# The input projection of a gated-convolution layer as seven half-size products for two output tiles

## The chip, the cores and the metric

One Trainium2 chip, of which the kernel uses one core. The metric is the device time of the core in microseconds (us); lower is better. A profile tells of one execution; the median is taken over several.

## The reference, cut to what matters

Two residual layers act on x, 512 positions of 2048 channels, all in float32, and a last RMSNorm follows. The first layer (delta rule heads beside windowed attention) is the same before and after. The change is in the second:

```python
def shortconv_layer(h, w_in, conv_w, w_out):
    gate_b, gate_c, u, z = jnp.split(h @ w_in, 4, axis=-1)       # w_in: 2048 x 4*3072
    y = gate_b * causal_depthwise_conv(gate_c * u, conv_w)        # 3 taps
    return (y * jax.nn.silu(z)) @ w_out                           # w_out: 3072 x 2048
...
    h = x + hybrid_layer(rmsnorm(x, norm_w[0]), ...)
    h = h + shortconv_layer(rmsnorm(h, norm_w[1]), ...)
    return rmsnorm(h, final_norm_w)
```

Computed are h @ w_in with 12288 output channels, that is 96 tiles of 128, then the gating and the convolution, then the output projection.

## The kernel before, in words

Activations lie transposed, channels on the 128 partitions and the 512 positions along the free dimension, so a tile is 128 x 512. A float32 product is made of three matmuls in the faster fp32r format: each operand is split into a high part (a copy, rounded to fp32r) and a low part (the difference), and hi*hi, hi*lo and lo*hi are added in PSUM (`mm3`, lines 146 to 151; the three matmuls are L148, L149 and L150). The weights are split as they come: SP loads 8 blocks of 128 x 128, 512 KB, into `w_raw` (two buffers), ACT makes `w_hi` (L141), DVE makes `w_lo` (L143; three buffers each). The activations are split once per layer.

The whole program, by TensorE: the first layer's input projection with the attention and delta-rule work in its gaps; its output projection `w1o` (16 tiles of 24 blocks); the second layer's input projection `w2` (24 steps c of four tiles, 16 blocks each: C, u, z, B); its output projection `w2o` (16 tiles of 24 blocks), whose last tile is done in two halves of 256 columns so that the end of the kernel is short.

The order on TensorE is that of the code (`manual_schedule`); small side tasks enter it by estimated times (`Flow`). On the other engines a scheduler orders the instructions by priority at build time, and each engine then works through its own list in order. Weight loads and splits have a raised priority (`SPLIT_AHEAD`), so that they run ahead as far as buffers allow.

In the loop over c (lines 786 to 809) a projected tile is in PSUM when DVE multiplies it by the norm factor `rbc`, forms the convolution, and at the end of a step makes y, which is split at once into `y_hi` and `y_lo` and kept for the output projection. The residual h1 of the first layer's output, needed again at the end, is stored in DRAM (`H1d`). The activations of the second layer are split by `split_x`, nine tiles as they come, the others from a reload during the last tile of `w1o`. No DMA is issued from POOL.

## Time and profile before

| | us |
|---|---|
| median of 3 runs | 2880.93 (2878.38 to 2881.74) |
| the profiled execution, its span | 2882.2 |
| TensorE busy in it | 2854.8 |
| DVE busy | 1429.0 |
| ACT busy | 877.5 |
| the 23 loop steps that the rows below take | 1012.5 |

The profiled execution's span lies 1.3 us above the median of the runs. Busy time of TensorE is modelled (matmuls overlap, each shows 0.39 us where the next one starts after 0.23), so the distance from one start to the next is the cost of a matmul, and the duration isn't. Weight loads (PEld) overlap them.

### The profile page before, as it was taken

To read this page: it belongs to the slowest core of one execution; us is meant where nothing else is said; L and a number is where in the kernel's file an instruction comes from. 1 tells how busy PE (TensorE), PEld (TensorE's weight loads), DVE (VectorE), ACT (ScalarE), POOL (GpSimd) and SP (SyncE) were. 2 spreads that over 40 slices of the span, in tenths; PEclk is the share of its full clock that TensorE was granted. 3 is DMA by queue.
4 is the path that set the end of the run, shared out by engine and by line. 5 is a ranking of instruction groups with operands and counts; after the bars stand their busy time and mean duration, and the time that the engine had idled before them with its cause. 6 is when DMAs were issued, how large, how long until landed. Compare 5 with 4: busy or idle time off the path is not lost.

```text
span 2882.2 us, 33247 instructions
## 1 busy us (share of the span) xinstructions
PE 2854.8 (99%) x13192; PEld 2362.8 (82%) x13192; DVE 1429.0 (50%) x2179; ACT 877.5 (30%) x1483; POOL 78.8 (3%) x130
## 2 busy tenths in 40 slices
...
GB/s 167 179 181 174 92 87 147 89 84 92 86 91 146 103 120 108 103 101 141 130 130 128 95 96 95 95 95 95 95 96 95 99 98 95 95 95 114 114 114 112
DMA packets 135515, 322.19 MB, mean 112 GB/s; under 512 B 38128, under 2 KB 52720, under 8 KB 135104
## 3 DMA queue, kind: packets, MB, share of 16 engines
...
## 4 chain that ended last, share of the span: by engine, by line
PE 95%; DVE 2%; DMA 1%; ACT 1%; issue 1%; SPq 0%; DVEq 0%; POOL 0%; ACTq 0%
PE acc L148 30%; PE acc L150 29%; PE acc L149 29%; PE p L94 2%; PE o_ps L94 1%; PE s_ps L482 0%; PE s_ps L481 0%; PE s_ps L483 0%; DVE w_lo L143 0%; PE vt_ps L98 0%; DVE y_lo L730 0%; PE kk_ps L94 0%; PE x_ps L94 0%; PE t_ps L94 0%; PE p_ps L98 0%
## 5 line engine op out<-in xcount | busy, mean ns | idle before, releaser
L148 PE MATMUL acc<-x_hi,w_hi 128*128 128x512 f32 x3072 | 1229.8, 400 | 1.7 <-DVE cv_raw L316 1.6
L150 PE MATMUL acc<-x_hi,w_lo 128*128 128x512 f32 x3072 | 1205.7, 392 | 5.0 <-DVE w_lo L143 2.8
L149 PE MATMUL acc<-x_lo,w_hi 128*128 128x512 f32 x3072 | 1200.1, 391 | 0.1
L141 ACT ACTIVATE w_hi<-w_raw 128x1024 fp32r<-128x1024 f32 (+2 forms) x494 | 513.1, 1039 | 1535.4 <-PE acc L149 1153.4
L143 DVE TENSOR_TENSOR w_lo<-w_raw,w_hi 128x1024 fp32r<-128x1024 f32 (+2 forms) x494 | 600.4, 1216 | 657.4 <-ACT w_hi L141 656.7
L150 PEld LDWEIGHTS acc<-x_hi,w_lo 128*128 128x128 f32 x3072 | 578.4, 188 | 137.2 <-DVE w_lo L143 5.4
L149 PEld LDWEIGHTS acc<-x_lo,w_hi 128*128 128x128 f32 x3072 | 579.7, 189 | 118.3 <-DVE x_lo L197 0.5
L148 PEld LDWEIGHTS acc<-x_hi,w_hi 128*128 128x128 f32 x3072 | 579.5, 189 | 116.6 <-DVE cv_raw L316 1.8
L148 PE MATMUL acc<-y_hi,w_hi 128*128 128x512 f32 (+1 forms) x792 | 304.5, 384 | 0.0
L150 PE MATMUL acc<-y_hi,w_lo 128*128 128x512 f32 (+1 forms) x792 | 303.4, 383 | 0.0
L149 PE MATMUL acc<-y_lo,w_hi 128*128 128x512 f32 (+1 forms) x792 | 303.4, 383 | 0.0
L149 PEld LDWEIGHTS acc<-y_lo,w_hi 128*128 128x128 f32 x792 | 149.0, 188 | 28.9
L148 PEld LDWEIGHTS acc<-y_hi,w_hi 128*128 128x128 f32 x792 | 149.0, 188 | 28.9
L150 PEld LDWEIGHTS acc<-y_hi,w_lo 128*128 128x128 f32 x792 | 149.0, 188 | 28.7
L320 DVE SCALAR_TENSOR_TENSOR cv<-cv_raw,dcw_sb,cv 128x512 f32<-128x512 f32 x96 | 71.6, 747 | 0.9
L493 ACT ACTIVATE sc<-sc,nb 128x128 f32<-128x128 f32 (+3 forms) x96 | 50.3, 526 | 47.4 <-DVE nb L491 47.2
L793 DVE TENSOR_TENSOR cu<-acc,cr 128x512 f32<-128x512 f32 x24 | 16.6, 692 | 81.8 <-PE acc L150 81.8
L801 DVE TENSOR_TENSOR zrs<-acc,rbc 128x512 f32<-128x512 f32 x24 | 16.6, 692 | 81.8 <-PE acc L150 81.8
L789 DVE TENSOR_TENSOR cr<-acc,rbc 128x512 f32<-128x512 f32 x24 | 16.6, 692 | 78.7 <-PE acc L150 78.7
L808 DVE SCALAR_TENSOR_TENSOR y<-acc,gzs 128x512 f32<-128x512 f32 x24 | 16.6, 692 | 77.3 <-PE acc L150 77.2
L430 DVE TENSOR_TENSOR itmp<-na 128x62 f32<-128x62 f32 (+30 forms) x62 | 52.8, 852 | 0.4
L432 DVE TENSOR_TENSOR na<-na,itmp 128x62 f32<-128x62 f32 (+30 forms) x62 | 52.8, 852 | 0.3
...
## 6 DMA issues: line engine op xcount, KB each, us to landing
w_raw<-in_w_dram SPq DMA_DIRECT2D x380, 512.0 KB, 3.5
w_raw<-in_w1o_dram SPq DMA_DIRECT2D x48, 512.0 KB, 3.6
w_raw<-in_w2o_dram SPq DMA_DIRECT2D x48, 512.0 KB, 3.6
xr<-in_xT_dram SPq DMA_DIRECT2D x16, 256.0 KB, 4.3
KQd<-kq SPq DMA_DIRECT2D x8, 512.0 KB, 5.1
dd<-Gd SPq DMA_DIRECT2D x16, 256.0 KB, 5.0
QKd<-aq SPq DMA_DIRECT2D x16, 256.0 KB, 2.9
kql<-KQd SPq DMA_DIRECT2D x8, 512.0 KB, 3.5
```

The lines of the kernel that those rows point to most:

```text
L94: PE.matmul(o, lhsT, rhs, start=start, stop=stop)
L141: A.activation(hi, raw, AF.Copy)
L143: V.tensor_sub(lo, raw, hi.bitcast(F32))
L148: PE.matmul(acc, hi, xh, start=first, stop=False)
L149: PE.matmul(acc, hi, xl, start=False, stop=False)
L150: PE.matmul(acc, lo, xh, start=False, stop=last)
L320: V.scalar_tensor_tensor(cv, raw[:, j:j + T], dcw_sb[:, ci, j:j + 1], cv, op0=ALU.mult, op1=ALU.add)
L430: V.tensor_tensor(tv, na[:, j:j + 1, j + 1:64].to_broadcast([P, j, w]), na[:, 0:j, j:j + 1].to_broadcast([P, j, w]), op=ALU.mult)
L432: V.tensor_tensor(na[:, 0:j, j + 1:64], na[:, 0:j, j + 1:64], tv, op=ALU.add)
L493: A.activation(scs[g], scs[g], AF.Exp, bias=nb, scale=SCALE, accum_out=den[:, g:g + 1])
L789: V.tensor_tensor(cr, acc, rbc2, op=ALU.mult)
L793: V.tensor_tensor(cu[:, 2:T + 2], acc, cr, op=ALU.mult)
```

## The change

The second layer's input projection is done for two output tiles at a time by Strassen's scheme in the form with 15 additions. The contraction is cut in two halves (even and odd blocks of 128 channels: `halves` in the host's layout), the positions in two halves of 256, and the two output tiles are the third pair. Seven products of 8 blocks with 256 columns replace two of 16 blocks with 512. Each product is again three matmuls (hi*hi, hi*lo, lo*hi).

For the activations, `forms` makes seven combinations of the four quadrants of a pair of tiles and splits each into hi and lo: 56 tiles in all, made once. Those of the block pairs 0 to 2 are made as the output projection of the first layer yields its tiles, of 3 to 6 during its last two tiles from a reload, of the last one at its end; the last two tiles are therefore computed together, block by block. For the weights, five raw tiles per pair are loaded; two of the four sums (s1, s3) are made by a transfer from POOL that adds into the loaded tile, two (on q11, on q12) by DVE. The seven weight matrices are split as before. Eight raw buffers replace two. Three PSUM tiles take the products, and DVE and ACT copy or add the parts out.

The 56 forms take the places in which y was kept (`xp` and `x2p`), and the six new raw buffers take the place of the y tiles of the first layer. So y is stored in DRAM (`Y2d`) and read back and split behind the loop, all but the last. The tap product of line 795 goes from DVE to ACT.

```diff
-NX2 = 9
+NX2 = 24
+NJ1 = 3
+NRAW = 6
...
+    Y2d = dram.tile([NCH, P, T], F32, name="Y2d")
...
-    xs2 = [None] * KT
...
-                    for k in range(KT - NX2):
-                        hr = op1.tile([P, T], F32, name="hr")
-                        SP.dma_start(hr, H1d[k])
-                        xs2[k] = split_x(*PX, hr, k, 1)
...
-            accA = proj(w2[0], xs2)
...
-                acc = accA if c == 0 else proj(w2[4 * c], xs2)
-                cr = sc.tile([P, T], F32, name="cr", tag="crz")
-                V.tensor_tensor(cr, acc, rbc2, op=ALU.mult)
-                acc = proj(w2[4 * c + 1], xs2)
-                cu = sc.tile([P, T + 2], F32, name="cu")
-                G.memset(cu[:, 0:2], 0.0)
-                V.tensor_tensor(cu[:, 2:T + 2], acc, cr, op=ALU.mult)
-                cv = sc.tile([P, T], F32, name="cvs")
-                V.tensor_scalar(cv, cu[:, 0:T], scw_sb[:, c, 0:1], None, op0=ALU.mult)
-                for j in range(1, 3):
...
-                ys.append(split_y(PX if c < NX2 or c >= NX2 + 12 else PYA if c < NX2 + 4 else PYD, yt))
+    slots = iter([(x2p, "x2", NX2)] * NX2 + [(xp, "x", 32)] * 32)
+    fm = [[None] * NJ for _ in range(7)]
+
+    def form(i, j, src):
+        pool, tag, bufs = next(slots)
+        t = pool.tile([P, 2, H], F32R, name="fm", tag=tag, bufs=bufs)
+        A.activation(t[:, 0, :], src, AF.Copy)
+        V.tensor_tensor(t[:, 1, :], src, t[:, 0, :].bitcast(F32), op=ALU.subtract)
+        fm[i][j] = (t[:, 0, :], t[:, 1, :])
+
+    def forms(pool, j, he, ho):
+        e1, e2, o1, o2 = he[:, 0:H], he[:, H:T], ho[:, 0:H], ho[:, H:T]
+        form(0, j, e1)
+        fa, fb = (pool.tile([P, H], F32, name=n) for n in ("fa", "fb"))
+        V.tensor_tensor(fa, e1, e2, op=ALU.subtract)
+        V.scalar_tensor_tensor(fb, fa, -1.0, o2, op0=ALU.mult, op1=ALU.subtract)
+        form(5, j, fb)
+        form(4, j, fa)
+        fc, fd = (pool.tile([P, H], F32, name=n) for n in ("fa", "fb"))
+        V.tensor_tensor(fc, e2, o2, op=ALU.subtract)
+        form(6, j, fc)
+        form(1, j, o1)
+        form(2, j, o2)
+        V.tensor_tensor(fd, o1, fb, op=ALU.add)
+        form(3, j, fd)
+
...
+            if m < 2 * NJ1 or m >= KT - 2:
+                scaled(m, h1)
+                if m % 2:
+                    forms(op1, m // 2, hs[m - 1], hs[m])
...
+        last = (KT - 2, KT - 1)
+        rxs = [residual(m) for m in last]
+        accs = [new_acc() for _ in last]
+        for c in range(KO // CK):
+            with tc.high_priority(offset=SPLIT_AHEAD):
+                ws = [load_split(wp, w1o[m][:, c * CK:(c + 1) * CK, :], CK) for m in last]
+            for i in range(CK):
+                k = c * CK + i
+                flow.poll()
+                for acc, (hi, lo) in zip(accs, ws):
+                    mm3(acc, hi[:, i, :], lo[:, i, :], ys[k], k == 0, k == KO - 1)
+        for j in range(NJ1, NJ - 1):
+            for m in (2 * j, 2 * j + 1):
+                hr = op1.tile([P, T], F32, name="hr", tag="hr")
+                SP.dma_start(hr, H1d[m])
+                scaled(m, hr)
+            forms(op1, j, hs[2 * j], hs[2 * j + 1])
+        for m, acc, rx in zip(last, accs, rxs):
+            made(m, acc, rx)
...
+    yds.close()
+    with tc.tile_pool(name="w4", bufs=1) as w4, tc.tile_pool(name="sc", bufs=1, side="right") as sc:
+
+        def raw():
+            i = nraw[0]
+            nraw[0] += 1
+            pool, tag, bufs = ((wp, "w_raw", 2), (w4, "w_raw4", NRAW))[i % (2 + NRAW) >= 2]
+            return pool.tile([P, NJ, P], F32, name="w_raw", tag=tag, bufs=bufs)
+
+        nraw = [0]
+
+        def split_w(src):
+            hi = wp.tile([P, NJ, P], F32R, name="w_hi", tag="w_hi", bufs=3)
+            A.activation(hi, src, AF.Copy)
+            lo = wp.tile([P, NJ, P], F32R, name="w_lo", tag="w_lo", bufs=3)
+            V.tensor_sub(lo, src, hi.bitcast(F32))
+            return hi, lo
+
+        def product(w, f, o, first):
+            hi, lo = w
+            o = o[:, 0:H]
+            for j in range(NJ):
+                flow.poll()
+                xh, xl = fm[f][j]
+                PE.matmul(o, hi[:, j, :], xh, start=first and j == 0, stop=False, skip_group_check=not first)
+                PE.matmul(o, hi[:, j, :], xl, start=False, stop=False, skip_group_check=not first)
+                PE.matmul(o, lo[:, j, :], xh, start=False, stop=j == NJ - 1, skip_group_check=not first)
+                flow.t += 0.36
+
+        def pair(wa, wb, c1, c2):
+            with tc.high_priority(offset=SPLIT_AHEAD):
+                q11, s1, s3, q12, q22 = (raw() for _ in range(5))
+                SP.dma_start(s1, wb[:, 0:NJ, :])
+                G.dma_start(s1, wb[:, NJ:KT, :], accum_op=ALU.add)
+                SP.dma_start(q11, wa[:, 0:NJ, :])
+                SP.dma_start(s3, wa[:, 0:NJ, :])
+                G.dma_start(s3, wb[:, 0:NJ, :], accum_op=ALU.add)
+                SP.dma_start(q12, wa[:, NJ:KT, :])
+                SP.dma_start(q22, wb[:, NJ:KT, :])
+            a, b, c = new_acc(), bank("sb"), bank("sc")
+            with tc.high_priority(offset=SPLIT_AHEAD):
+                w = split_w(q11)
+            product(w, 0, a, True)
+            a1 = sc.tile([P, H], F32, name="a1", bufs=2)
+            A.activation(a1, a[:, 0:H], AF.Copy)
+            with tc.high_priority(offset=SPLIT_AHEAD):
+                V.tensor_tensor(q11, q11, s1, op=ALU.add)
+                w = split_w(q11)
+            product(w, 5, b, True)
+            e = sc.tile([P, H], F32, name="e", bufs=2)
+            V.tensor_tensor(e, b[:, 0:H], a1, op=ALU.add)
+            with tc.high_priority(offset=SPLIT_AHEAD):
+                w = split_w(s3)
+            product(w, 6, c, True)
+            with tc.high_priority(offset=SPLIT_AHEAD):
+                w = split_w(s1)
+            product(w, 4, b, False)
+            b2 = sc.tile([P, H], F32, name="b2", bufs=1)
+            V.tensor_tensor(b2, b[:, 0:H], a1, op=ALU.add)
+            V.tensor_tensor(c2[:, H:T], c[:, 0:H], b2, op=ALU.subtract)
+            with tc.high_priority(offset=SPLIT_AHEAD):
+                w = split_w(q12)
+            product(w, 1, a, False)
+            A.activation(c1[:, 0:H], a[:, 0:H], AF.Copy)
+            with tc.high_priority(offset=SPLIT_AHEAD):
+                V.tensor_tensor(q12, q12, q11, op=ALU.add)
+                w = split_w(q12)
+            product(w, 2, b, False)
+            V.tensor_tensor(c1[:, H:T], b[:, 0:H], a1, op=ALU.add)
+            with tc.high_priority(offset=SPLIT_AHEAD):
+                w = split_w(q22)
+            product(w, 3, c, False)
+            V.tensor_tensor(c2[:, 0:H], c[:, 0:H], e, op=ALU.subtract)
...
+            pair(w2[4 * c], w2[4 * c + 1], cc, u)
+            if c == 0:
+                flow.drain()
+                V.tensor_tensor(rbc2, rbc, rbc, op=ALU.mult)
+            V.tensor_tensor(u, u, cc, op=ALU.mult)
+            V.tensor_tensor(u, u, rbc2, op=ALU.mult)
+            A.activation(cc, cu[:, 0:T], AF.Copy, scale=scw_sb[:, c, 0:1])
+            for j in range(1, 3):
+                V.scalar_tensor_tensor(cc, cu[:, j:j + T], scw_sb[:, c, j:j + 1], cc, op0=ALU.mult, op1=ALU.add)
+            V.tensor_tensor(cc, cc, rbc, op=ALU.mult)
+            cz, cb = ctile(), ctile()
+            pair(w2[4 * c + 2], w2[4 * c + 3], cz, cb)
+            V.tensor_tensor(cz, cz, rbc, op=ALU.mult)
+            gz = sc.tile([P, T], F32, name="gzs")
+            A.activation(gz, cz, AF.Tanh, scale=0.5)
+            V.scalar_tensor_tensor(gz, gz, 1.0, cz, op0=ALU.add, op1=ALU.mult)
+            V.tensor_tensor(gz, gz, cc, op=ALU.mult)
+            yt = sc.tile([P, T], F32, name="y2", bufs=2)
+            V.scalar_tensor_tensor(yt, cb, 0.5, gz, op0=ALU.mult, op1=ALU.mult)
+            if c < NCH - 1:
+                SP.dma_start(Y2d[c], yt)
+        ys = [None] * NCH
+        for c in range(NCH):
+            if c < NCH - 1:
+                yl = sc.tile([P, T], F32, name="yl", tag="ct", bufs=6)
+                SP.dma_start(yl, Y2d[c])
+            else:
+                yl = yt
+            ys[c] = split_y(PX if c < 16 else (x2p, "x2", NX2), yl)
...
+    halves = np.arange(DM).reshape(KT // 2, 2, P).transpose(1, 0, 2).reshape(-1)
+    w2 = mtiles(sc_w_in[0][halves], np.concatenate(```

The order of instructions shows it at three places. First DVE within one step of the loop, from the step's first operation on, as it was; `w_lo` are the weight splits, L789 to L798 the pointwise work:

```order
L789 TENSOR_TENSOR cr<-acc,rbc_12703 128x512 [waits PE_49]
L143 TENSOR_TENSOR w_lo<-w_raw,w_hi 128x1024 [waits DMAHW3_49,Activation_49]
L143 TENSOR_TENSOR w_lo<-w_raw,w_hi 128x1024 [waits DMAHW4_49,PE_49,Activation_49]
L793 TENSOR_TENSOR cu<-acc,cr 128x512 [waits DVE_49,PE_49]
L795 TENSOR_SCALAR cvs<-cu,scw_sb 128x512 [waits DVE_49,Pool_49]
L143 TENSOR_TENSOR w_lo<-w_raw,w_hi 128x1024 [waits DMAHW5_49,Activation_49]
L797 SCALAR_TENSOR_TENSOR cvs<-cu,scw_sb,cvs 128x512 [waits DVE_49] x2
L798 TENSOR_TENSOR cvs<-cvs,rbc 128x512 [waits DVE_49]
```

And DVE now, in a pair that follows one of C and u, from the combination that waits for the pair before to the sixth product's weights; L888 to L910 are combinations of products, `ct` the tiles they make, L903 the sum of weights on DVE:

```order
L910 TENSOR_TENSOR ct<-sc,e 128x256 [waits PE_49]
L853 TENSOR_TENSOR w_lo<-w_raw,w_hi 128x1024 [waits DMASW7_49,Activation_49]
L924 TENSOR_TENSOR ct<-ct 128x512 [waits DVE_49]
L925 TENSOR_TENSOR ct<-ct,rbc_12831 128x512 [waits DVE_49]
L853 TENSOR_TENSOR w_lo<-w_raw,w_hi 128x1024 [waits PE_49,Activation_49]
L928 SCALAR_TENSOR_TENSOR ct<-ct,scw_sb 128x512 [waits Activation_49]
L888 TENSOR_TENSOR e<-sb,a_13590 128x256 [waits PE_49]
L928 SCALAR_TENSOR_TENSOR ct<-ct,scw_sb 128x512 [waits DVE_49]
L853 TENSOR_TENSOR w_lo<-w_raw,w_hi 128x1024 [waits DMAHW2_49,Activation_49]
L929 TENSOR_TENSOR ct<-ct,rbc 128x512 [waits DVE_49]
L903 TENSOR_TENSOR w_raw<-w_raw 128x1024 [waits DVE_49]
L896 TENSOR_TENSOR b_13679<-sb,a_13590 128x256 [waits PE_49]
```

The splits now stand between operations that wait for single products (PE in the brackets), and two of a pair's splits stand behind a transfer of POOL (DMASW).

Second SP's queue where the loop is entered. It was, from the last reloads of h1 on:

```order
L139 DMA w_raw<-in_w_dram 128x1024 [waits DMAHW2_49,DVE_49]
L768 DMA hr<-H1d 128x512 [waits DMAHW6_49,DMAHW1_49,DVE_49]
L775 DMA H1d<-h_12614 128x512 [waits DVE_49]
L139 DMA w_raw<-in_w_dram 128x1024 [waits DMAHW5_49,DVE_49]
L139 DMA w_raw<-in_w_dram 128x1024 [waits DMAHW0_49,DVE_49]
```

It is now (L870 to L876 are the loads of s1, q11, s3, q12 and q22 of the first pair and the next):

```order
L142 DMA w_raw<-in_w1o_dram 128x1024 [waits DMAHW4_49,DVE_49]
L870 DMA w_raw<-in_w_dram 128x1024 [waits DMAHW5_49,DVE_49]
L831 DMA hr<-H1d 128x512 [waits DMAHW2_49,Activation_49]
L872 DMA w_raw<-in_w_dram 128x1024 [waits DMAHW4_49,DVE_49]
L873 DMA w_raw<-in_w_dram 128x1024 [waits PE_49]
L875 DMA w_raw<-in_w_dram 128x1024
L876 DMA w_raw<-in_w_dram 128x1024
L870 DMA w_raw<-in_w_dram 128x1024 [waits DMAHW3_49]
```

The load of s3 (L873) waits for TensorE, whose reads of the first layer's y end there, and the loads behind it wait with it.

Third DVE where the loop is left. It was (L804 to L808 end the last step, L820 is the first output tile's sum):

```order
L805 TENSOR_TENSOR gzs<-gzs,cvs 128x512 [waits DVE_49]
L143 TENSOR_TENSOR w_lo<-w_raw,w_hi 128x1024 [waits DMAHW0_49,PE_49,Activation_49]
L808 SCALAR_TENSOR_TENSOR y_19022<-acc,gzs 128x512 [waits DVE_49,PE_49]
L143 TENSOR_TENSOR w_lo<-w_raw,w_hi 128x1024 [waits DMAHW1_49,Activation_49]
L730 TENSOR_TENSOR y_lo<-y_19022,y_hi 128x512 [waits Activation_49]
L143 TENSOR_TENSOR w_lo<-w_raw,w_hi 128x1024 [waits DMAHW2_49,PE_49,Activation_49]
L143 TENSOR_TENSOR w_lo<-w_raw,w_hi 128x1024 [waits DMAHW3_49,PE_49,Activation_49]
L820 TENSOR_TENSOR h_19136<-acc,rx_19043 128x512 [waits DMAHW4_49,DVE_49,PE_49]
```

It is now (`yl` are tiles read back; L910 waits for the last product):

```order
L734 TENSOR_TENSOR y_lo<-yl,y_hi 128x512 [waits DMAHW2_49,Activation_49]
L734 TENSOR_TENSOR y_lo<-yl,y_hi 128x512 [waits DMAHW3_49,Activation_49]
L910 TENSOR_TENSOR ct<-sc,e 128x256 [waits PE_49]
L146 TENSOR_TENSOR w_lo<-w_raw,w_hi 128x1024 [waits DMAHW4_49,Activation_49]
L935 SCALAR_TENSOR_TENSOR gzs<-gzs,ct 128x512 [waits Activation_49]
L734 TENSOR_TENSOR y_lo<-yl,y_hi 128x512 [waits DMAHW5_49,Activation_49]
L936 TENSOR_TENSOR gzs<-gzs,ct 128x512 [waits DVE_49]
L734 TENSOR_TENSOR y_lo<-yl,y_hi 128x512 [waits DMAHW7_49,Activation_49]
L734 TENSOR_TENSOR y_lo<-yl,y_hi 128x512 [waits DMAHW0_49,Activation_49]
L938 SCALAR_TENSOR_TENSOR y_24005<-ct,gzs 128x512 [waits DVE_49]
L734 TENSOR_TENSOR y_lo<-yl,y_hi 128x512 [waits DMAHW2_49,Activation_49]
```

Three y tiles are split before L910, one of them above the piece shown; the other 21 stand behind it.

## Rows read from the trace of the kernel before

**Rows 1.** The page: busy time of each engine, and the chain that ended last, by engine
```profile
PE 2854.8 (99%) x13192; PEld 2362.8 (82%) x13192; DVE 1429.0 (50%) x2179; ACT 877.5 (30%) x1483; POOL 78.8 (3%) x130
PE 95%; DVE 2%; DMA 1%; ACT 1%; issue 1%; SPq 0%; DVEq 0%; POOL 0%; ACTq 0%
```

**Rows 2.** Windows, the 23 steps of the layer's loop: busy us, clock, DMA share, GB/s
```profile
1558.60:2571.10 1012.50, 1012.50 (x4417) 829.94 (x4416) 388.49 (x434) 218.49 (x229) 2.29 (x23) 1.00 0.29 96
```

**Rows 3.** Line 789, first op of each loop step: count, ns min/median/max, first and last start
```profile
L789 DVE TENSOR_TENSOR cr<-acc,rbc x24: 691/692/692, 1558.6 to 2571.1; 128x512 f32<-128x512 f32 x24
```

**Rows 4.** Waits in 1640 to 2640 us: SP's queue, then DVE (us, times, longest)
```profile
SPq L139 <- DVE w_lo L143: 917.9, 182, 5.4
DVE w_lo L143 <- ACT w_hi L141: 311.4, 160, 4.3
DVE cu L793 <- PE acc L150: 74.9, 22, 3.4
```

**Rows 5.** Timeline of TensorE, 256-column products of the last output tile, 20 L148 starts
```profile
2852.77 0.28 PE L148 MATMUL acc<-y_hi,w_hi 128*128 128x256 f32 x1
...
2859.61 0.28 PE L148 MATMUL acc<-y_hi,w_hi 128*128 128x256 f32 x1
```

**Rows 6.** Timeline of TensorE, 512-column products, eight L148 starts: start us, us
```profile
2839.98 0.39 PE L148 MATMUL acc<-y_hi,w_hi 128*128 128x512 f32 x1
...
2844.74 0.39 PE L148 MATMUL acc<-y_hi,w_hi 128*128 128x512 f32 x1
```

**Rows 7.** Windows, the 256-column stretch: busy us of PE, PEld, DVE, ACT, POOL
```profile
2853.00:2859.00 6.00, 6.00 (x52) 6.00 (x51) 0.42 (x1) 0.82 (x2) 0.00 (x0) 1.00 0.01 3
```

**Rows 8.** Groups by shape, DVE and ACT: xcount, busy us, mean ns of one, idle before
```profile
L143 DVE TENSOR_TENSOR w_lo<-w_raw,w_hi 128x1024 fp32r<-128x1024 f32 x476 | 582.6, 1224 | 656.9 <-ACT w_hi L141 656.2
L141 ACT ACTIVATE w_hi<-w_raw 128x1024 fp32r<-128x1024 f32 x476 | 504.8, 1061 | 1534.1 <-PE acc L149 1152.6 <-issue 346.0 <-DMA w_raw<-in_w_dram 7.2
L370 DVE TENSOR_TENSOR aq<-kk,dd 128x1024 f32<-128x1024 f32 x16 | 18.9, 1218 | 0.4 <-ACT kk L359 0.4
L797 DVE SCALAR_TENSOR_TENSOR cvs<-cu,scw_sb,cvs 128x512 f32<-128x512 f32 x48 | 36.0, 749 | 0.8
L798 DVE TENSOR_TENSOR cvs<-cvs,rbc 128x512 f32<-128x512 f32 x24 | 16.6, 692 | 0.8
L730 DVE TENSOR_TENSOR y_lo<-y,y_hi 128x512 fp32r<-128x512 f32 x24 | 16.4, 685 | 0.8 <-ACT y_hi L728 0.8
L651 DVE TENSOR_TENSOR vs<-p,c 128x256 f32<-128x256 f32 x24 | 10.1, 423 | 19.5 <-PE p L94 19.4
L498 DVE TENSOR_TENSOR sc<-sc,sc 128x256 f32<-128x256 f32 x24 | 9.9, 414 | 0.0
L654 ACT ACTIVATE vn<-p 128x256 f32<-128x256 f32 x32 | 12.3, 383 | 63.3 <-DVE vs L651 52.2 <-PE p L94 11.0
L803 ACT ACTIVATE gzs<-zrs 128x512 f32<-128x512 f32 x24 | 15.0, 625 | 0.0
```

**Rows 9.** DMA issues: KB each, median us from issue to landing
```profile
w_raw<-in_w_dram SPq DMA_DIRECT2D x380, 512.0 KB, 3.5
T11d<-itmp SPq DMA_DIRECT2D x4, 512.0 KB, 6.2
yl<-YBd SPq DMA_DIRECT2D x8, 256.0 KB, 3.1
hr<-H1d SPq DMA_DIRECT2D x7, 256.0 KB, 3.9
```

**Rows 10.** Groups, the longest operation of POOL
```profile
L223 POOL TENSOR_TENSOR ssq<-ssq,sq 128x512 f32<-128x512 f32 x16 | 23.7, 1480 | 17.9 <-ACT sq L222 17.7
```

**Rows 11.** Windows around the one long pause of TensorE between its large products
```profile
863.00:868.00 5.00, 2.40 (x17) 1.82 (x15) 2.77 (x4) 1.54 (x2) 0.65 (x3) 0.93 0.23 70
868.00:873.00 5.00, 5.00 (x12) 3.94 (x13) 4.21 (x11) 1.26 (x2) 0.32 (x2) 0.50 0.95 311
```

75 lines of the change are left out of this document (35 added, 40 removed).

## The prediction

> **What bounds the kernel now.** I read the page first: TensorE is busy 99% of the span, and the chain that ended last lies on PE for 95% of it [rows 1]. Then the windows over the loop that the change rewrites: in 1012.5 us TensorE has no idle time at all, DVE is busy 388 us, ACT 218 us, POOL 2 us, the DMA engines 29% [rows 2]. The first operation of a loop step starts at 1558.6 us for the first and at 2571.1 us for the last of 24 steps [rows 3], so a step takes 1012.5 / 23 = 44.02 us, for 4 x 48 = 192 matmuls of 512 columns: 0.2293 us each. The reader is to see in the waits that the others wait for TensorE or for one that does: SP's loads for DVE to free the raw weights, 917.9 us in all, DVE for ACT's weight splits and for the products' ends [rows 4]. So in this loop the time is the number of matmuls times the step from one to the next, and nothing else ends last. All 24 steps cost 24 x 44.02 = 1056.5 us.
>
> **The change part by part.**
>
> *The products.* Each two output tiles took 2 x 48 matmuls of 512 columns; now seven products of 8 x 3 matmuls of 256 columns, 168. In all 4608 matmuls go and 48 x 168 = 8064 come. What a half-width matmul costs is shown by the last output tile, which is done in two halves: from the first to the last of 20 starts of line 148, 57 matmuls apart, 6.84 us, 0.1200 us each [rows 5]. The 512-column ones of the output projection take 4.76 / 21 = 0.2267 us [rows 6]. So half the columns cost 53% of the time, not 50%, and of Strassen's eighth (7/8) only 7/8 x 2 x 0.1200 / 0.2267 = 0.926 is left. 8064 x 0.1200 = 967.7 us. The stretch of rows 5 has DVE, ACT and DMA nearly idle, and its weight loads fill all 6.00 of 6.00 us [rows 7]; in the loop they will be busy. The nearest row for that: the loop's 512-column step is 0.2293 [rows 2], where the output projection's is 0.2267 [rows 6], 1.15% more. With that share on top it is 978.9 us. I take the middle, 973.3 us. The gain on TensorE is 1056.5 - 973.3 = 83.2 us, 77.6 to 88.8.
>
> *Does DVE keep up?* Per pair of tiles DVE now has seven w_lo splits of 1024 elements at 1.224 us, two weight sums of that size at 1.218, five combinations of 256 columns at 0.423, and half of a step's pointwise work: seven operations of 512 columns at 0.69 and two multiply-adds at 0.749 [rows 8]. That is 8.57 + 2.44 + 2.12 + 3.16 = 16.3 us, against 168 x 0.1207 = 20.3 us of TensorE: 80%, where it was 38%. ACT: 7 x 1.061 + 2 x 0.383 + 0.625 = 8.8 us, 43% [rows 8]. Both are covered, if the order of the queues lets them run ahead. I followed DVE's order through one pair with those durations, from the end T of the pair before. Weight buffers are three, so product n's split begins when product n-3 ends (products take 2.9 us). The w_lo of the third product is ready at T + 2.3 and wanted at T + 5.8; the fourth 5.2 and 8.7; the fifth 8.3 and 11.6; the seventh 14.8 and 17.4; the next pair's first two 16.7 and 20.3, 20.3 and 23.2. The tightest is the sixth, whose weights are summed on DVE only after the fifth's split: split, line 929, sum, ACT's copy, line 896, split end at T + 13.2, wanted at T + 14.5. Even that has 1.3 us. Cost in the loop: nothing, covered by TensorE; if the cover goes, see the second rival.
>
> *The loads.* Per pair seven transfers of 512 KB in place of four, two of them adding into their target from POOL's queue, plus half a store of y: 3.8 MB per 20.3 us, 188 GB/s (96 now [rows 2]). An adding transfer isn't in this trace. Lower bound: a plain load, 3.5 us to landing; upper: that load plus the slowest 512 KB row, 3.5 + 6.2 = 9.7 us [rows 9]; what POOL needs to issue one is bounded by nothing and its longest operation, 1.48 us [rows 10]. I take 6.2 us plus 1.5. The raw buffers are eight for five per pair: s1 of a pair may load some 24 us before it is needed, s3 26 us, q12 and q22 17 us or more before. Load plus adding, 3.5 + 7.7 = 11.2 us (14.7 at the upper bound), hides in that, and two per pair fit in 20.3 us even one after the other.
>
> *Entering the loop* costs TensorE, since it was seamless before. Let T be the end of the last output-projection matmul. (a) The first product has seven of eight k-blocks ready, 21 x 0.12 = 2.5 us of cover. For the eighth DVE still does, in its order, two residual adds (0.69 each, the first from T - 0.5), one w_lo, two adds into ssq and four operations of 256 columns: 1.38 + 1.22 + 1.37 + 1.66 - 0.5 = 5.1 us [rows 8], so 2.6 us late. (b) The third product's weights s3 lie where the pool of y tiles was, whose last reader is the projection's last block: the load is issued at T, lands at T + 3.8, the adding one at T + 11.5, split T + 13.8; wanted at T + 2.6 + 5.8 = 8.4. 5.4 us late. (c) The last two projection tiles run interleaved with three weight buffers for pairs: at the first border the second tile's split is ready about 0.6 us late. (d) Such pauses can halve the clock: after 2.6 idle us in 863 to 868 us the granted clock stood at 0.50 (1.2 GHz) for the next 5 us [rows 11]; that would cost about 2.5 us here. Together 11 us.
>
> *Leaving the loop.* The y tiles no longer split as they come; 23 are stored and read back, since their place is held by the forms until the last product. DVE's order puts three of them before the last product's combination, so behind it 21 splits at 0.685, four operations of the last step and three w_lo come to 14.4 + 2.5 + 3.7 = 20.6 us [rows 8], and three matmuls, 0.7 us, follow the last of them. The first output tile takes 72 x 0.2267 = 16.3 us when nothing holds it: 5 us late. Reloading (3.1 to 3.9 us each [rows 9], at first three buffers) adds perhaps 1 us. Together 6 us.
>
> The forms' other work (77 operations of 256 columns on DVE, 0.414 each [rows 8]) lies beside the output projection, where TensorE ends last; nothing is charged.
>
> Sum: 2882.2 (profiled span) - 83.2 + 11 + 6 = 2816.0. The median of the runs shown, 2880.93, is 1.3 us under that span, so 2814.7; I say 2815. The forecast's own range: gain 77.6 to 88.8, ends together 5 to 30 us (both late sums hidden by work done earlier, or both doubled by the clock): 2797 to 2833.
>
> **The rivals.**
> 1. *The adding loads become the bound* (slower). Everything in a pair waits for s1 and s3. If POOL's queue does its two adding transfers one after the other and one takes x us, a pair takes at least 2x. The change breaks even when a pair loses (83.2 - 17) / 48 = 1.38 us, at 21.65 us: x = 10.8 us decides. At 13 us, 26 per pair, the kernel ends at 2815 + 48 x 5.7 = 3089 us. For: no adding transfer and no DMA of POOL is in the trace. Against: the upper bound of 9.7 us from rows 9, and 0.95 of DMA share was reached at 311 GB/s [rows 11]. Chance 8%. The Trainium skill, "SBUF — State Buffer", section "Who interferes with whom", would raise it: the descriptors of a transfer issued from POOL can't be written while DVE runs an operation that takes both of its ports, as copies and tensor_scalar do. By the same section tensor_tensor takes no such mode, and the loop's one tensor_scalar, line 795, became ACT's line 926; no run here shows either.
> 2. *DVE becomes the bound in the loop.* If its operations come 30% slower beside twice the DMA traffic and POOL's transfers, 16.3 us become 21.2 a pair, 0.9 us over TensorE's, lost 48 times: 2815 + 43 = 2858 us. For: it is busy 80%, in order, and waits for TensorE within each pair. Against: the margins above, and 1.3 us of the tightest one is not eaten by less than a third. Chance 9%.
> 3. *Half-width matmuls are slower among busy engines*, by 5%: 0.126 us, 1016 us, the gain 40: 2858 us. For: weight loads fill rows 7. Against: with twice the columns the load made 1.15%. Chance 5%.
> 4. *Half the columns cost half*, 0.1133 us [rows 6]: 914 us, 2815 - 59 = 2756 us. For: nothing but arithmetic. Against: rows 5, at the full granted clock of 1.00 [rows 7]. Chance 4%. The Trainium skill, "TensorE: Matmul & The Clock Gate", section "Back-to-back issue gap", goes further, columns / 2.4 GHz + 2.5 ns, an estimate of 109.2 ns for 256 columns, and the loop would take 881 us; the trace's 120 ns disagree, and the measurement decides.
>
> **How the numbers follow.** Forecast 74%, rivals 8, 9, 5 and 4%. Low end: 2795, just under the forecast's best case, which leaves rival 4 out. High end: 2860, which takes in rivals 2 and 3 at their prices and leaves out 1. What a measurement can tell from no change is 0.2%, 5.8 us. Faster by more than that: 74 + 9 + 5 + 4 = 92%, less 2 for rivals 2 and 3 at double price, 90%; within 0.2%: 2%; slower: 8%.
>
> **What would show it.** TensorE's starts 0.120 to 0.1215 us apart within a product, the loop's step at 40.5 us from one line 924 to the next, PE without waits inside the loop, DVE near 80% there. Idle time of TensorE before the first and third product of the first pair, and in the first output tile, line by line behind y_lo. Wrong would be: PE waiting for w_hi or w_lo in every pair (rival 2), DVE or ACT waiting for an adding transfer in every pair (rival 1), or starts over 0.125 us apart (rival 3).

## The result and the profile after

2818.02 us, median of 4 runs (2814.83 to 2821.60), against 2881.34 for the kernel before in the same comparison: a ratio of 0.9783, interval 0.9769 to 0.9797. The forecast was 2815, so the sum came out. Its terms did not: the gain on TensorE was larger, and so was what entering and leaving the loop cost, by nearly as much. That the two errors cancelled is luck.

The stages show it. They are cut at TensorE's first matmul on a y tile, its first of the second layer's input projection and its first of the second output projection (timelines of both traces; us):

| stage | before | after | moved by | forecast |
|---|---|---|---|---|
| up to the first y matmul | 1277.39 | 1276.46 | -0.9 | 0 |
| first output projection | 268.21 | 273.50 | +5.3 | part of the entry's +11 |
| input projection, 24 steps | 1058.37 | 976.61 | -81.8 | -83.2, and the rest of the +11 |
| from the first y matmul after it to the end | 278.19 | 293.27 | +15.1 | +6 |
| span | 2882.16 | 2819.84 | -62.3 | -66 |

The page's busy times and its chain answer to [rows 1]: TensorE is busy 98% of the span and is still what ends last, with 93% of that chain; DVE is at 64% for 50, and POOL's work has doubled by issuing adding loads.

```profile
PE 2774.8 (98%) x16648; PEld 2463.6 (87%) x16648; DVE 1798.9 (64%) x2707; ACT 1091.6 (39%) x1803; POOL 160.6 (6%) x226
PE 93%; DVE 3%; DMA 2%; issue 1%; ACT 1%; SPq 0%; DVEq 0%; POOL 0%; ACTq 0%; POOLq 0%
```

The window over the changed loop, from line 924 of the first step to that of the last (columns as in [rows 2]), and the starts of that line, which answer to [rows 3]:

```profile
1586.70:2508.90 922.20, 922.20 (x7730) 922.20 (x7730) 713.07 (x853) 395.01 (x460) 80.07 (x112) 1.00 0.71 190
```

```profile
L924 DVE TENSOR_TENSOR ct<-ct x24: 685/686/690, 1586.7 to 2508.9; 128x512 f32<-128x512 f32 x24
```

TensorE never waits there; its weight loads are full now too, DVE is at 77%, the DMA engines at 71% where they were at 29%. A step takes 922.2 / 23 = 40.10 us for 336 matmuls, 0.1193 us each: below the 0.1200 that I had as the lower bound. 8064 of these are 962.3 us; the stage's other 14.3 us lie at its start. In 1600 to 2500 us the others wait for TensorE or for one that does, as in [rows 4]:

```profile
ACT w_hi L851 <- PE acc L863: 156.8, 87, 1.8
DVE w_lo L853 <- ACT w_hi L851: 141.4, 202, 1.5
```

DVE's operations kept their lengths, and an adding load takes 7.1 us in the middle; these answer to [rows 8, 9, 10], first the groups of the loop by shape, then the issues (KB, median us to landing), then what an adding load takes POOL to issue:

```profile
L853 DVE TENSOR_TENSOR w_lo<-w_raw,w_hi 128x1024 fp32r<-128x1024 f32 x308 | 376.9, 1224 | 139.8 <-ACT w_hi L851 138.1
L884 DVE TENSOR_TENSOR w_raw<-w_raw 128x1024 f32<-128x1024 f32 x44 | 53.9, 1225 | 1.5
L896 DVE TENSOR_TENSOR b<-sb,a 128x256 f32<-128x256 f32 x44 | 18.6, 422 | 38.1 <-PE sb L864 38.1
```

```profile
w_raw<-in_w_dram SPq DMA_DIRECT2D x428, 512.0 KB, 4.4
w_raw<-in_w_dram POOLq DMA_DIRECT2D x96, 512.0 KB, 7.1
Y2d<-y SPq DMA_DIRECT2D x23, 256.0 KB, 5.3
yl<-Y2d SPq DMA_DIRECT2D x23, 256.0 KB, 4.4
```

```profile
L871 POOL DMA_DIRECT2D w_raw<-in_w_dram x48: 857/862/1056, 1533.6 to 2476.7; - x48
```

At the entry all of TensorE's waits, 1515 to 1575 us (us, times, longest), and then windows behind the pauses, the first behind that at the border, the others from the first product on (the granted clock is the third number from the end):

```profile
PE sc L862 <- ACT w_hi L851: 5.5, 1, 5.5
PE acc L151 <- ACT w_hi L144: 1.6, 1, 1.6
PE acc L863 <- DVE fm L769: 1.3, 1, 1.3
PE acc L153 <- DVE w_lo L146: 1.2, 2, 0.9
PE sc L864 <- DVE w_lo L853: 0.5, 1, 0.5
PE acc L862 <- ACT fm L768: 0.3, 1, 0.3
```

```profile
1525.00:1530.00 5.00, 3.83 (x11) 2.71 (x12) 5.00 (x12) 4.88 (x12) 0.00 (x0) 0.76 0.58 189
1550.00:1560.00 10.00, 8.42 (x56) 8.02 (x55) 7.04 (x17) 4.84 (x12) 1.06 (x2) 0.83 0.84 273
1560.00:1570.00 10.00, 4.07 (x18) 3.57 (x18) 4.21 (x5) 3.33 (x4) 2.75 (x4) 0.76 1.06 256
1570.00:1580.00 10.00, 10.00 (x79) 10.00 (x78) 4.88 (x7) 3.94 (x5) 0.86 (x1) 0.90 0.88 273
```

The waits are those forecast: the third product for s3 (L862 into sc), the eighth block of forms (L768, L769), the border of the interleaved tiles (L151, L153). What the 5.5 us are made of, the chain of waits says (start, us): the load of s3, issued when the projection ends, and the adding load behind it, 9.79 us beside five other loads at a DMA share of 1.06, then ACT's split.

```profile
1550.15 4.14 DMA w_raw<-in_w_dram
...
1554.83 9.79 DMA w_raw<-in_w_dram
...
1564.70 1.06 ACT w_hi L851
1565.79 1.24 DVE w_lo L853
```

At the exit, 2526 to 2555 us, waits of TensorE and of ACT:

```profile
PE acc L152 <- DVE y_lo L734: 3.5, 7, 0.9
PE acc L151 <- ACT y_hi L732: 3.2, 4, 1.3
```

```profile
ACT y_hi L732 <- DMA yl<-Y2d: 9.0, 6, 3.0
```

TensorE waits for splits of y, as forecast, but the splits wait 9.0 us for reloads. That is another cause than mine, which was DVE's turn; experiment 4 tells the two apart.

### The profile page after: what moved, and what is told of

Its sections match the earlier page's. It is cut to its first block, busy times and chain, and to the rows that moved or that the text cites. A ratio compares the mean times of both kernels' runs of the same rounds, so it can differ in the third digit from the quotient of the medians.

```text
span 2819.8 us, 41852 instructions
## 1 busy us (share of the span) xinstructions
PE 2774.8 (98%) x16648; PEld 2463.6 (87%) x16648; DVE 1798.9 (64%) x2707; ACT 1091.6 (39%) x1803; POOL 160.6 (6%) x226
## 3 DMA queue, kind: packets, MB, share of 16 engines
q0 software_dynamic: 13824, 50.34, 10.1%
## 4 chain that ended last, share of the span: by engine, by line
PE 93%; DVE 3%; DMA 2%; issue 1%; ACT 1%; SPq 0%; DVEq 0%; POOL 0%; ACTq 0%; POOLq 0%
PE acc L151 17%; PE acc L153 17%; PE acc L152 17%; PE sb L862 5%; PE sb L864 5%; PE sb L863 5%; PE sc L862 3%; PE sc L864 3%; PE acc L862 3%; PE acc L864 3%; PE sc L863 3%; PE acc L863 3%; PE p L96 2%; DMA w_raw<-in_w_dram 1%; DVE w_lo L146 1%
## 5 line engine op out<-in xcount | busy, mean ns | idle before, releaser
L151 PE MATMUL acc<-x_hi,w_hi 128*128 128x512 f32 x1536 | 622.5, 405 | 1.6 <-DVE cv_raw L319 1.6
L153 PE MATMUL acc<-x_hi,w_lo 128*128 128x512 f32 x1536 | 602.3, 392 | 5.1 <-DVE w_lo L146 5.1
L152 PE MATMUL acc<-x_lo,w_hi 128*128 128x512 f32 x1536 | 600.6, 391 | 0.5 <-DVE x_lo L200 0.3
L144 ACT ACTIVATE w_hi<-w_raw 128x1024 fp32r<-128x1024 f32 (+2 forms) x302 | 308.9, 1024 | 683.9 <-PE acc L152 513.9
L851 ACT ACTIVATE w_hi<-w_raw 128x1024 fp32r<-128x1024 f32 x336 | 356.3, 1061 | 559.2 <-PE acc L863 165.8
L146 DVE TENSOR_TENSOR w_lo<-w_raw,w_hi 128x1024 fp32r<-128x1024 f32 (+2 forms) x302 | 363.6, 1206 | 315.1 <-ACT w_hi L144 314.4
L853 DVE TENSOR_TENSOR w_lo<-w_raw,w_hi 128x1024 fp32r<-128x1024 f32 x336 | 411.0, 1224 | 160.9 <-ACT w_hi L851 159.0
L153 PEld LDWEIGHTS acc<-x_hi,w_lo 128*128 128x128 f32 x1536 | 289.2, 188 | 69.6 <-DVE w_lo L146 7.2
L151 PEld LDWEIGHTS acc<-x_hi,w_hi 128*128 128x128 f32 x1536 | 290.1, 189 | 57.4 <-DVE cv_raw L319 1.8
L152 PEld LDWEIGHTS acc<-x_lo,w_hi 128*128 128x128 f32 x1536 | 290.3, 189 | 55.8 <-DVE x_lo L200 1.8
L862 PE MATMUL sb<-fm,w_hi 128*128 128x256 f32 x1152 | 325.9, 283 | 0.0
L864 PE MATMUL sb<-fm,w_lo 128*128 128x256 f32 x1152 | 325.2, 282 | 0.0
L863 PE MATMUL sb<-fm,w_hi 128*128 128x256 f32 x1152 | 324.5, 282 | 0.0
L151 PE MATMUL acc<-y_hi,w_hi 128*128 128x512 f32 (+1 forms) x792 | 307.6, 388 | 4.8 <-ACT y_hi L732 3.2
L152 PE MATMUL acc<-y_lo,w_hi 128*128 128x512 f32 (+1 forms) x792 | 305.7, 386 | 3.5 <-DVE y_lo L734 3.5
L153 PE MATMUL acc<-y_hi,w_lo 128*128 128x512 f32 (+1 forms) x792 | 305.8, 386 | 1.2 <-DVE w_lo L146 1.2
L862 PE MATMUL sc<-fm,w_hi 128*128 128x256 f32 x768 | 218.0, 284 | 5.5 <-ACT w_hi L851 5.5
L862 PEld LDWEIGHTS sb<-fm,w_hi 128*128 128x128 f32 x1152 | 219.7, 191 | 0.0
L863 PEld LDWEIGHTS sb<-fm,w_hi 128*128 128x128 f32 x1152 | 218.9, 190 | 0.0
L864 PEld LDWEIGHTS sb<-fm,w_lo 128*128 128x128 f32 x1152 | 218.5, 190 | 0.0
L864 PE MATMUL sc<-fm,w_lo 128*128 128x256 f32 x768 | 217.5, 283 | 0.5 <-DVE w_lo L853 0.5
L863 PE MATMUL acc<-fm,w_hi 128*128 128x256 f32 x768 | 216.0, 281 | 1.3 <-DVE fm L769 1.3
## 6 DMA issues: line engine op xcount, KB each, us to landing
w_raw<-in_w_dram SPq DMA_DIRECT2D x428, 512.0 KB, 4.4
w_raw<-in_w_dram POOLq DMA_DIRECT2D x96, 512.0 KB, 7.1
w_raw<-in_w1o_dram SPq DMA_DIRECT2D x48, 512.0 KB, 3.6
w_raw<-in_w2o_dram SPq DMA_DIRECT2D x48, 512.0 KB, 3.6
Y2d<-y SPq DMA_DIRECT2D x23, 256.0 KB, 5.3
yl<-Y2d SPq DMA_DIRECT2D x23, 256.0 KB, 4.4
xr<-in_xT_dram SPq DMA_DIRECT2D x16, 256.0 KB, 4.3
KQd<-kq SPq DMA_DIRECT2D x8, 512.0 KB, 5.1
```

Source lines behind the costliest of these rows:

```text
L144: A.activation(hi, raw, AF.Copy)
L146: V.tensor_sub(lo, raw, hi.bitcast(F32))
L151: PE.matmul(acc, hi, xh, start=first, stop=False)
L152: PE.matmul(acc, hi, xl, start=False, stop=False)
L153: PE.matmul(acc, lo, xh, start=False, stop=last)
L851: A.activation(hi, src, AF.Copy)
```

## The experiments

Each was made from the changed kernel, the first from the kernel before. Stage lengths are cut as above.

**1. Half-width matmuls with the old placement and traffic.**

```
-                mm3(acc, hi[:, j, :], lo[:, j, :], xs[k], ...)
+                for s in (slice(0, 256), slice(256, 512)):
+                    PE.matmul(acc[:, s], hi[:, j, :], xh[:, s], ...)  # hi*xl, lo*xh alike
```

> The kernel before, with each 512-column matmul of the second input projection (line 148 to 150) done as two of 256 columns: 9216 in place of 4608, all else as before, and the result the same. It prices the half-width step with the old placement of the operands and the old traffic. Theory A (the shape sets it; what made the 512-column step 0.2297 us in this loop doesn't touch half-width ones): 9216 x 0.1193 = 1099.5 us for the loop in place of 1058.4, the span 2882 + 41 = 2923 us, PEld full. Rival (the loop's share of 1.15% goes on top, as half of my sum had it): 9216 x 0.1214 = 1118.8 us, the span 2943 us.

This kernel does not keep the result, and its first tile stays at 512 columns; the other 9120 matmuls are as said. The stage took 1096.39 us, the span 2918.2 us (timed once: 2919.94): theory A. Inside the loop a matmul takes 1000 / 8418 = 0.1188 us, with DVE, ACT and DMA as busy as in the kernel before:

```profile
1600.00:2600.00 1000.00, 1000.00 (x8418) 1000.00 (x8417) 370.20 (x414) 207.47 (x217) 2.19 (x22) 1.00 0.28 93
```

The 1.15% that the 512-column step had in this loop doesn't touch the half-width one. From start to start the step is 120.0 ns for the blocks of activations in xp and 117.8 for those in x2p, as in the changed kernel.

**2. Without the adding loads.**

```
-                G.dma_start(s1, wb[:, NJ:KT, :], accum_op=ALU.add)
...
-                G.dma_start(s3, wb[:, 0:NJ, :], accum_op=ALU.add)
```

> The changed kernel without its two accumulating loads per pair: s1 and s3 are only loaded, so the weight sums are left out and the products are those of other weights. Theory A (the adding loads cost only at the first pair, where s3 waits for load plus adding load): the idle 5.75 us before the first pair's third product shrinks to under 0.5 us, the clock there stays higher, the loop's step stays at 40.1 us, the span falls from 2819.8 to 2810 us, give or take 3. Rival (rival 1 of the prediction in a mild form: the adding loads also cost in every pair): the step of the loop falls by over 0.2 us, 48 half steps or 5 us more.

2809.33 us (one run), span 2807.5. The loop stage fell by 8.5 us, all at its start: the wait for s3 is gone, TensorE's longest wait there is 1.3 us, and the window 1620 to 2500 us holds the same number of matmuls as in the changed kernel (7377, shown under 9 and 10), with the DMA share at 0.42 for 0.71:

```profile
1620.00:2500.00 880.00, 880.00 (x7377) 880.00 (x7377) 680.07 (x813) 376.03 (x438) 2.08 (x21) 1.00 0.42 139
```

So 96 adding loads cost nothing but at the first pair. Theory A; the other 4 us by which the span fell lie in stages that this edit doesn't touch.

**3. The second tile four blocks behind.**

```
+        for s in range(KO + CK // 2):
+            for n, k in enumerate((s, s - CK // 2)):   # tile n at block k
+                mm3(accs[n], ws[n][0][:, k % CK, :], ws[n][1][:, k % CK, :], ys[k], ...)
```

> The changed kernel with the last two tiles of the output projection still interleaved, but the second running four k-blocks behind the first, so that their weight splits do not want the three weight buffers at the same border. Theory A (the borders cost the ring's wait and the clock after it): the projection from its first matmul to the first product takes 268 to 269 us, not 273.5, the time falls by 4 to 6 us. Rival (TensorE stops at 1523 us because ACT and DVE are full of forms, whichever buffer is free): the stops stay, and the time moves by less than 1.5 us.

Both are wrong in part. The pauses are gone and the projection takes 268.19 us, as before the change: theory A's mechanism. But the time is 2818.33 us (ratio 0.9781, interval 0.9766 to 0.9796), no change that can be told, and in the trace 2.0 of the 5.3 us come back in the loop stage (978.62 us). The wait for s3 grows from 5.5 to 11.1 us:

```profile
PE sc L864 <- ACT w_hi L853: 11.1, 1, 11.1
```

s3 does come earlier. Its load hangs on the end of the projection: the adding load landed 14.4 us behind that end (at 1557.85 us), in the changed kernel 14.7 us (at 1564.62). What has changed is that the first two products now run without a pause and end 3.3 us sooner after it; that time TensorE waits for the third. Another 2.3 us are new: in ACT's queue the split of s3 stands behind the copy of the first product (L884), and by the chain of waits that copy was released by a store of h1 that took 13.51 us to land:

```profile
1546.63 13.51 DMA H1d<-rx
...
1560.52 1.06 ACT w_hi L853
```

**4. Other buffers for the reloads.**

```
-                yl = sc.tile([P, T], F32, name="yl", tag="ct", bufs=6)
-                SP.dma_start(yl, Y2d[c])
...
+                yl = w4.tile([P, 2, T], F32, name="yl", tag="w_raw4", bufs=NRAW)   # every other c
...
+                SP.dma_start(yl[:, 0:n, :], Y2d[c:c + n].rearrange("c p t -> p c t"))
```

> The changed kernel with the reloaded y tiles in the six raw weight buffers of 4 KB, two y to a buffer and to a load (12 loads of 512 KB, the last of 256 KB), in place of the six buffers of 2 KB that the pointwise tiles held; the splits and their places stay. Theory A (the exit waits for reloads that wait for buffers): TensorE's idle 9.7 us in the first output tile falls under 3 us, from the first matmul on y to the end it takes 280 to 283 us in place of 293.3, the time falls by 10 to 13 us. Rival (the prediction's account: DVE's 21 splits behind the last product are what is late): the stops stay between 4 and 8 us, and the time falls by no more than 5 us.

2809.22 us (ratio 0.9751, 0.9734 to 0.9767), 8.8 less. The exit took 279.97 us for 293.27 and TensorE has no wait at its start (2526 to 2560 us): theory A, the reloads were the cause. That the loads also doubled in size doesn't matter: experiment 11 loads the tiles one by one into the same buffers and its exit takes 280.47 us. Not all of the gain stays, because splits now come before the last products' weights in ACT's queue and wait there for a reload, 2.27 us with two weight splits behind them:

```profile
2519.09 0.63 ACT L732 ACTIVATE y_hi<-yl 128x512 fp32r<-128x512 f32 x1 [2.27 <-DMA yl<-Y2d]
2519.63 1.99 ACT L851 ACTIVATE w_hi<-w_raw 128x1024 fp32r<-128x1024 f32 x2
```

**5. The sums on DVE.**

```
-                G.dma_start(s1, ..., accum_op=ALU.add); SP.dma_start(s3, ...); G.dma_start(s3, ..., accum_op=ALU.add)
+                V.tensor_tensor(s3, q11, s1, op=ALU.add)
+                V.tensor_tensor(s1, s1, q22, op=ALU.add)
...   # and the loads come in the order q11, s1, q22, q12
```

> The changed kernel with the weight sums s1 and s3 made by DVE from the plain loads (s3 from q11 and the first half of the second tile, so it needs no load of its own): four loads of 512 KB per pair in place of seven, none adding, and two more operations of 1024 elements on DVE. Theory A (the adding loads cost at the entry only, and DVE has the room): DVE's busy share in the loop goes from 77% (713 of 922 us) to (15.5 + 2.44) / 20.05 = 89%, the step of the loop stays at 40.1 us, the 5.75 us of idle time before the first pair's third product goes, and the time falls to 2808 to 2811 us. Rival (rival 2 of the prediction, DVE in order becomes the bound near 90%): TensorE waits for w_hi or w_lo in every pair, the step is over 40.5 us and the time 2828 us or more.

2818.82 us (ratio 0.9787, 0.9773 to 0.9802). In the loop theory A holds: the profile shows no wait of TensorE, with DVE at 88%.

```profile
1620.00:2500.00 880.00, 880.00 (x7365) 879.03 (x7364) 770.03 (x899) 371.67 (x438) 2.10 (x21) 1.00 0.35 112
```

The 12 matmuls fewer than in the changed kernel, 1.4 us, lie before the sixth product, whose weights the prediction had found the tightest. The time did not fall, against theory A, because at the entry DVE's sum of s1 waits for the load of q22, and the last forms stand behind it: 3.6 us for forms, 3.1 for the split behind the first product, 2.5 for the normaliser's operation on POOL, which itself waited for DVE, in place of the 5.5.

**6. The sums on POOL.** The same edit with POOL in place of DVE.

> As the kernel with DVE's sums, but both sums on POOL, which is otherwise idle in the loop: at 1.44 us for 512 elements in this trace about 2.9 us each, 5.8 of a pair's 20 us. Theory A (POOL's sums lie beside everything, wanted a pair ahead): step 40.1 us, the entry without the 5.75 us, 2808 to 2811 us. Rival (POOL's sums hold up DVE's operations or come too late at the entry): DVE's w_lo of 1224 ns become longer than 1300 ns on average, or TensorE waits before each pair's second and third product; the step is over 40.3 us and the time no better than 2815 us.

2852.08 us (ratio 0.9904, 0.9887 to 0.9920): the rival, and worse than it said. POOL's sums took 2.3 to 4.7 us, and those of DVE's operations on two SBUF operands that ran beside one grew. Operations that read PSUM did not:

```profile
L853 DVE TENSOR_TENSOR w_lo<-w_raw,w_hi 128x1024 fp32r<-128x1024 f32 x298 | 452.0, 1522 | 70.5 <-ACT w_hi L851 61.9 <-PE acc L863 7.2
L927 DVE SCALAR_TENSOR_TENSOR ct<-ct,scw_sb 128x512 f32<-128x512 f32 x42 | 49.4, 1177 | 0.0
L895 DVE TENSOR_TENSOR b<-sb,a 128x256 f32<-128x256 f32 x42 | 17.5, 416 | 18.9 <-PE sb L864 18.9
```

1522 ns on average for 1224, and 416 for 422. By the starts and ends in the trace, 1600 to 2500 us, the 64 splits that overlap a sum of POOL took 2644 ns on average, the other 241 took 1220. The Trainium skill, "SBUF — State Buffer", section "Who interferes with whom", has the rule: a DVE instruction with two SBUF inputs contends with a GpSimd (here POOL) instruction that reads SBUF. This trace agrees. DVE at 88% without POOL beside it (experiment 5) costs 1.4 us; with it the loop stage is 1011.71 us for 981.38, 30 more.

**7. Another order in the first pair.** s1 and s3 go into the two buffers that are free early; their products come first.

```
+            product(ws1, 4, b, True, range(NJ - 1))
+            product(ws3, 6, c, True, range(NJ - 1))
+            product(ws1, 4, b, True, (NJ - 1,))
+            product(ws3, 6, c, True, (NJ - 1,))
+            ...   # then q11's products 0 and 5, then 1, 2, 3 as before
```

> The changed kernel with another order in the first pair only: the products of s1 and s3 come first, both loaded and summed by adding loads into the two buffers that are free before the projection ends, their last k-blocks after the first seven of both, then q11's; adding loads stay in all pairs. Theory A (what the entry costs is that the third product's weights can only be loaded after the projection, and the late eighth block of forms): the pauses of 1.5 us and 5.75 us go, at most 2 us of new ones come before q11's product, TensorE's clock stays up, the loop from its first product to its last falls from 976.6 to 966 to 970 us, the time to 2808 to 2812 us. Rival (the loads crowd the queues at that place, whatever waits for them: q11 and q12 arrive as late as s3 did): the pause moves to q11's or q12's product, and the time stays within 3 us of 2818.

2811.21 us (ratio 0.9762, 0.9748 to 0.9777), the loop stage 968.83: theory A. What is left at the loop's start is one wait for the forms, and one for the normaliser's task, which was behind POOL's queue:

```profile
PE rs_pb L96 <- POOL rs_k L188: 3.2, 1, 3.2
PE sb L863 <- DVE fm L769: 0.9, 1, 0.9
```

**8. Three of them together.** Stagger, order and buffers, and `yield 10.0` for `yield 2.5` in the normaliser's task.

> The changed kernel with the stagger of the last two projection tiles, the first pair's other order and the reloads into the raw weight buffers together, and the second half of the normaliser's task 10 steps of the planner after the first in place of 2.5, so that TensorE does not meet it before POOL has its result (3.52 us of waiting in the kernel with the other order). Theory A (the losses at entry and exit are apart from one another and none hands its wait on): the projection at 268 us (from 273.5), the loop at 966 us (968.7 there, less 3), the exit at 280 us (from 293.3): 1276 + 268 + 966 + 280 = 2790 us, and 2 us more for the splits that come in the way of the last products: 2792, give or take 4. Rival (what the stagger alone showed: a pause removed ahead of the adding loads only comes back behind them): the 5 us of the projection come back in the loop, 2797 us or more.

2799.48 us (ratio 0.9720, 0.9706 to 0.9735). The projection 268.20 and the exit 280.01 are theory A's. The loop, 974.82, is 6.0 us longer than in experiment 7, and the time is the rival's. By the starts in both traces some 2.4 of the 6.0 us lie at the loop's end, where splits of y come in the way, which theory A had counted as 2; 3.6 lie at its start. There the wait for the normaliser's task is gone, and these have come (1515 to 1590 us):

```profile
PE sb L864 <- ACT e L932: 2.2, 1, 2.2
PE rs_ps L96 <- DVE ssq L807: 1.8, 1, 1.8
PE acc L864 <- ACT w_hi L853: 1.1, 1, 1.1
PE acc L866 <- DVE w_lo L855: 0.8, 1, 0.8
```

The first is the copy that frees the bank of the first product, the others are the normaliser's sums and the split of q11. For these the projection, which ends 5 us sooner, leaves less time; that is argued and not tested.

**9 and 10. 64 bytes.** The matmul's moving operand is here the tile of activations; weights and activations lie at some byte address in each partition, and what counts below is that address modulo 128. An unused tile moves what lies behind it; in 9 it stands ahead of the weight buffers and xp, in 10 between them.

```
     wp = ctx.enter_context(tc.tile_pool(name="wp", bufs=3))
+    ctx.enter_context(tc.tile_pool(name="gap", bufs=1)).tile([P, 16], F32, name="gap")
     xp = ctx.enter_context(tc.tile_pool(name="xp", bufs=1))
```

> The changed kernel with one unused tile of 64 bytes per partition ahead of the weight buffers and the pool xp, so that all that lies behind it in the low half of the memory moves by 64 bytes, and nothing else. In the changed kernel the step is 117.5 ns where the forms lie in x2p (byte address 32 modulo 128, the high half) and 120.0 ns in xp (96 modulo 128, as the weights, the low half). Theory A (the moving operand's place modulo 128 sets it): all forms are at 32 now, the step is 117.5 ns everywhere, the loop 8064 x (0.1193 - 0.1175) = 14 us shorter, the time about 2804 us. Rival 1 (a clash of the moving operand with weights of the same residue): all have the same residue now, 120.0 ns everywhere, 2823 us. Rival 2 (the half of the memory sets it): 117.5 and 120.0 as before, 2818 us.

> The changed kernel with the unused 64 bytes per partition between the weight buffers and the pool xp: the weights stay at byte address 96 modulo 128, all forms are at 32. The run before had all at 32, and all steps at 120.0 ns. Theory A (it is the same residue of weights and moving operand that costs the 2.5 ns, whatever it is): 117.5 ns for all forms, the loop's step 40.1 - 336 x 0.0018 = 39.5 us, the loop 14 us shorter, the time 2801 to 2806 us. Rival (the residue of the weights sets it: 96 is good with 32, but any clash is by the pool's distance): the forms in xp stay at 120.0 ns, 2818 us.

2822.01 us (ratio 0.9796, 0.9779 to 0.9812) and 2812.52 (0.9764, 0.9748 to 0.9780). The same 880 us of the loop, the changed kernel, 9, 10:

```profile
1620.00:2500.00 880.00, 880.00 (x7377) 880.00 (x7376) 681.26 (x813) 376.70 (x439) 77.48 (x109) 1.00 0.71 191
```

```profile
1620.00:2500.00 880.00, 880.00 (x7336) 880.00 (x7335) 677.34 (x810) 375.15 (x437) 77.49 (x109) 1.00 0.71 190
```

```profile
1620.00:2500.00 880.00, 880.00 (x7474) 880.00 (x7473) 688.14 (x823) 381.18 (x444) 78.36 (x110) 1.00 0.72 193
```

880 us over the counts gives 119.3, 120.0 and 117.7 ns: rival 1 of run 9 and theory A of run 10. In these kernels the address at which the moving operand lies against the weights sets the step of a half-width matmul. For 512 columns it is the other way round: in the first output projection 226.7 ns in 9 (two starts, 45 matmuls apart) and 228.8 in 10 (42 apart):

```profile
1459.64 0.39 PE L152 MATMUL acc<-y_hi,w_hi 128*128 128x512 f32 x1
...
1469.84 0.39 PE L152 MATMUL acc<-y_hi,w_hi 128*128 128x512 f32 x1
```

```profile
1460.04 0.39 PE L152 MATMUL acc<-y_hi,w_hi 128*128 128x512 f32 x1
...
1469.65 0.39 PE L152 MATMUL acc<-y_hi,w_hi 128*128 128x512 f32 x1
```

The time of 10 fell by 5.5 us and not by the 12 to 17 of its theory A, although the loop stage of its trace fell by 12.9; the rest of that gap stays open. The loop of the kernel before fits the two steps, 0.2293 against 0.2267 us in [rows 2, 6]: nine of its sixteen x tiles lay in x2p, at another address modulo 128 than its weights. By the starts in its trace these nine take 229.0 ns, most of those in xp 226.8, and the first blocks behind a change from one to the other up to 234.5.

**11. All of it.** Experiment 8 with the 64 bytes of 10, the first pair's product of q11 + s1 in a PSUM bank of its own, the normaliser's task five steps later, single reloads.

> The combined kernel with the 64 bytes between the weights and xp, the first pair's fourth product in a PSUM bank of its own (so that nothing has to be copied out of the bank before it), the normaliser's task 5 steps later, and the y tiles reloaded one by one into the halves of the raw buffers. Theory A (the terms add up): the projection at 268 us, the loop at 8064 x 0.1175 + 5 = 953 us, the exit at 280 us, 1275 + 268 + 953 + 280 = 2776 us, give or take 5. Rival (the 64 bytes move the 512-column stages the other way, since their operands lie behind them too): the first 1275 us grow by over 3 us, and the time stays over 2782 us.

2793.95 us (ratio 0.9695, 0.9680 to 0.9709), span 2788.0: the first stage took 1278.82 us and the projection 270.64, so the rival. The loop stage took 958.03, 5 us over theory A's sum too.

**12. Weights moved in the loop alone.**

```
-            hi = wp.tile([P, NJ, P], F32R, name="w_hi", tag="w_hi", bufs=3)   # lo alike
+            hl = wp.tile([P, 2 * NJ * P + 32], F32R, name="w_hl", tag="w_hl", bufs=3)
+            hi, lo = (hl[:, o:o + NJ * P].rearrange("p (j c) -> p j c", j=NJ) for o in (16, 16 + NJ * P))
```

> The kernel of the last combined run without the 64 bytes ahead of xp; all operands lie at byte address 96 modulo 128 now (x2p is moved by 64 bytes too), and only the loop's split weights are written 64 bytes further into their buffers, at 32. So the 512-column matmuls have both operands at one residue, the 256-column ones of the loop at two. To make room, the two split halves share a buffer and two small constants are loaded later. Theory A (the residues' effect has opposite signs: 226.7 ns with one residue and 228.9 with two for 512 columns, 120.0 and 117.5 for 256): the loop stays at 958 us, the first 1278.6 us fall to 1275, the projection's 270.4 to 268, the exit's 280.5 to 278; the span goes from 2788 to 2778 us, give or take 4, the time from 2794 to 2784. Rival (what the earlier stages lost in the last combined run was chance from run to run, and not the 512-column step): the time stays within 3 us of 2794.

2773.10 us, median of 5 runs (2769.90 to 2775.24), ratio 0.9623 (0.9610 to 0.9636): 11 us better than expected, and the fastest of all. But not by theory A, which fails at both ends. The loop stage fell to 926.68 us, not 958:

```profile
1620.00:2500.00 880.00, 877.29 (x7696) 875.17 (x7696) 716.47 (x868) 405.88 (x481) 78.57 (x110) 1.00 0.75 201
```

A step is 113.3 ns now, from these two starts, 78 matmuls apart:

```profile
1700.06 0.28 PE L864 MATMUL acc<-fm,w_hl 128*128 128x256 f32 x1
...
1708.90 0.28 PE L864 MATMUL acc<-fm,w_hl 128*128 128x256 f32 x1
```

And the stages with 512 columns grew: 1291.12, 273.08 and 282.60 us, at 230.7 ns a step in the first output projection, where 226.7 was expected. In this kernel the two split halves share a buffer of 8320 bytes, so the three buffers lie at three addresses modulo 512, where in all others they lay at one. So it is not the address modulo 128 alone. Which bits it is, and whether it matters that the halves are next to one another, stays open; so does a kernel with 113.3 ns in the loop and 226.7 in the rest.

## Why the prediction was right, and where it was not

**TensorE's gain** was 1058.4 - 962.3 = 96 us, forecast 83.2 (77.6 to 88.8): outside its bounds. The step that failed is "With that share on top it is 978.9 us. I take the middle": I carried the 1.15% by which the loop's 512-column matmuls were slower over to the half-width ones as the mark of busy engines. Experiment 1 shows that it isn't: with the same busy engines they take 0.1188. It was a matter of place (9, 10), and at half width the place works the other way: the forms in x2p take 117.8 ns, less than the 120.0 of [rows 5]. Of the 11.0 us between 973.3 and 962.3, 5.6 are that share and 5.4 the 0.1200, which was no lower bound; the rest of the 13 is that 1058.4 also holds the normaliser's small matmuls, where the prediction had 1056.5 for the steps alone.

**Entering the loop** cost 5.3 + 14.3 = 19.6 us, forecast 11. By its parts, from one start of TensorE to the next: (a) the late form block 2.0 us, forecast 2.6; (b) s3, 6.4 with the split behind it, forecast 5.4; (c) the interleaved tiles' borders 3.3, forecast 0.6, because ACT also had forms ahead of the weights, which I had left out. Of the other 8 us between 6 and 7 are steps at a lower clock, forecast 2.5 in (d): not one but three pauses were followed by it, and the windows show 0.76 behind the first and 0.83, 0.76 and 0.90 behind the others. The last 1.6 us are the normaliser's 16 small matmuls, which the stage before held too. The mechanisms were right, the sizes of (c) and (d) not: the forms' work beside the projection, for which "nothing is charged", was in the way of the weights. That (b) is an arrival and not a cost to be added up, experiment 3 showed: what TensorE saves between the end of the projection and that arrival, it waits there.

**Leaving the loop** cost 15.1 us, forecast 6. The step that failed is "behind it 21 splits ... 5 us late. Reloading ... adds perhaps 1 us": the reloads, six buffers of which the pointwise tiles held several, were the cause (experiment 4: other buffers, the splits as they were, and 13.3 us of the stage went); DVE had time. A further 2 us of the 15 are the step of 512 columns, 228.4 ns on average in the second output projection for 226.7 before, since eight of its 24 y tiles now lie in x2p.

**DVE and the adding loads** were hidden, as forecast: rival 1's price is 7.1 us in the middle, under the 10.8 that decide, and its two per pair come to 14 of 20.05 us; experiment 2 finds no cost in the loop. Rival 2's condition was not met: DVE's operations kept their lengths beside the traffic and took 15.5 us a pair, and even at 88% it cost 1.4 us in the loop (experiment 5). What makes it the bound is a POOL that reads SBUF beside it (experiment 6). Rival 3 is out, the step was shorter than 0.1200 us and not longer; rival 4 too, though its argument against, [rows 5], was a matter of place as well: the kernel of experiment 12 has the 113.3 ns, in another layout of the weights.

So 2815 stood 3 us from 2818 because 13 us too little gain met 18 us too little cost at the ends, which is luck. The range held the total; the range of the first term did not hold that term.
